# Encoder trunk: low weight parts of the input blocks by ScalarE and an accumulating DMA instead of a VectorE subtraction

## The chip, the cores and the metric

One core of a Trainium2 chip runs the whole program in one launch. The metric is device microseconds of one execution. Before the change it is 1680.81 us, the median of three runs (1680.68 to 1682.55).

## The reference

Two layers of a streaming encoder trunk run over 656 tokens (16 learned and 512 prompt tokens, and 8 running streams of 16). Each layer does

```
h    = rmsnorm(x, g_mix)
proj = h @ w_in                      # 1024 -> 3072: 24 blocks of 128 columns, the heads' inputs
oa   = diff_attention(qa, ka, va)    # 4 heads, two softmaxes each, chunk mask, cached keys
ob   = silu(layernorm(dwconv31(glu)))  # 256 channels, 31 taps
oc   = hgrn2(q, log_f, k, v, S0)     # 4 heads, 64x64 state
x    = x + concat(oa, ob, oc) @ w_out
x    = x + (gelu(dwconv3(gate)) * val) @ w_down   # gate, val = rmsnorm(x, g_ffn) @ w_up
```

All of it is float32. The change touches the weights of `h @ w_in` alone.

## The kernel before

**Split products.** TensorE multiplies in fp32r, which keeps fewer bits than float32. So each operand is split into a high part `hi`, its copy in fp32r, and a low part `lo = x - hi`, and `mm3` (L392) issues three matmuls for each 128x128 weight unit and each half of the tokens (328 columns): `whi` with `hi`, `whi` with `lo`, `wlo` with `hi`. One block of 128 output columns has 8 units and 2 token halves, so 48 matmuls. The first token half (24 matmuls) runs before the second; the low part of unit 4, the first unit of the second weight half, is read by matmul 15 of 48.

**Weights of a block.** `w_load` (L364) loads 128x1024 values (512 KB) into one of 4 `raw` buffers through SP's queue. `w_split` (L373) splits them in two halves of 128x512. For each half ScalarE copies `raw` to `whi` (L384), and VectorE writes `wlo = raw - whi` (L385). There are 4 pairs of `whi` and `wlo` buffers, so two blocks fit: a pair comes free when the block that used it has passed its last matmul on that half, and holds the same half of the block after next in order.

**Heads stage.** In each layer the first three blocks are computed together; then a loop runs over blocks n = 3 to 23 (L1188 on): product of block n (`gemm`, result `d_i` in PSUM), eviction by VectorE with the row factor (`evict_r`, L423), `weights` of block n + 1, and between them a step of each generator that has its inputs: the two HGRN2 pairs, the four attention heads (`front`), and the conv module (`back`). The stage is 42 to 311 us in the first layer and 870 to 1137 us in the second.

**Who fills which engine there.** VectorE has the conv's taps as two instructions each (L715 and L716, 18 of the 31 taps after the first), the evictions, the low parts, the masks and merges of HGRN2 and the softmax sums. ScalarE has the high parts, exponentials, squares and PSUM copies. Twelve conv taps per channel tile are made by ScalarE (`cvt`, L722 and L723) and summed by DMAs with `accum_op` add, issued by GpSimd (L725). GpSimd also scales the softmax rows (L528), builds block operands of the streams (`qx`, L644) and does some sums and clears.

**What sets the order.** No order is written out in this stage. A planner replays the program on a model of the engines' costs and gives each engine, in its free moments, the earliest instruction of the program whose inputs are ready; each engine, and each queue of DMA issues, then runs that list in order. So a changed instruction changes the lists of all engines in the stage. In the feed-forward part VectorE and TensorE follow an order that is written out.

Of the kernel before, what the change touches and what calls it, by code (L numbers as in the profile page):

```python
# [9 lines left out]
F32 = mybir.dt.float32  # L10
# [3 lines left out]
ALU = mybir.AluOpType  # L14
# [145 lines left out]
def trunk_kernel(ctx: ExitStack, tc: tile.TileContext, i: dict, o: dict, depth: int = 2):  # L160
# [12 lines left out]
    V, A, G, PE = nc.vector, nc.scalar, nc.gpsimd, nc.tensor  # L173
# [172 lines left out]
    def seq(ins):  # L346

        if start["on"]:
            tc.keep_in_program_order(ins)
            start[ins.ins.engine] = ins.ins  # L350
# [13 lines left out]
    def w_load(w, k0, kt, parts=None):  # L364
        raw = wraw.tile([128, 8, 128], F32, tag="raw", name="raw")
        for a, b in parts or ((0, kt),):
            nc.sync.dma_start(out=raw[:, a:b], in_=w[:, (k0 + a) * 128:(k0 + b) * 128].rearrange("p (k n) -> p k n", n=128))
        return raw

    def unit_s(name):  # L370
        return S(name, F32R)[:, :512].rearrange("p (k n) -> p k n", n=128)

    def w_split(raw, kt, a=0, own=False):  # L373

        half = 4 if kt in (4, 8) else 3
        units = []
        while a < kt:
            n = min(half, kt - a)
            if own:
                hi, lo = unit_s("ghi"), unit_s("glo")  # L380
            else:
                hi = wsp.tile([128, 4, 128], F32R, tag="whi", name="whi")
                lo = wsp.tile([128, 4, 128], F32R, tag="wlo", name="wlo")
            seq(A.copy(hi[:, :n], raw[:, a:a + n]))  # L384
            seq(V.tensor_tensor(out=lo[:, :n], in0=raw[:, a:a + n], in1=hi[:, :n].bitcast(F32), op=ALU.subtract))  # L385
            units += [(hi, lo, m) for m in range(n)]
            a += n
        return units

    def weights(w, k0, kt, own=False):  # L390
        return w_split(w_load(w, k0, kt), kt, 0, own)

    def mm3(ps, unit, rr, ab, first, last):
        whi, wlo, n = unit
# [11 lines left out]
    def gemm(units, ks, rhs, nm, cc=CA, P=PD):  # L406

        return [gemm1(units, ks, rhs, f"{c}_{nm}", cc[c], P) for c in range(2)]
# [11 lines left out]
    def evict_r(ps, r, nm):  # L420
        t = SE(nm)
        for c, (a, b) in enumerate(CA):
            V.tensor_tensor(out=t[:, a:b], in0=ps[c][:, :b - a], in1=r[:, a:b], op=ALU.mult)  # L423
        return t
# [712 lines left out]
    for l in range(depth):  # L1137
        w = i["w_in"][l]
# [3 lines left out]
        col = [cols[a] // 128 + b for a, b in order]  # L1142
        xsrc = i["x"] if l == 0 else xdr
        got, mix = {}, {}
        if l == 0:
            hs = []
            nc.sync.dma_start(out=xs[0][:, :T], in_=i["x"][0])
            raws = [w_load(w[col[n]], 0, 8, ((0, 4),)) for n in range(3)]
            for m in range(1, 4):
                nc.sync.dma_start(out=xs[m][:, :T], in_=i["x"][m])  # L1150
            for n in range(3):
                nc.sync.dma_start(out=raws[n][:, 4:], in_=w[col[n], :, 512:].rearrange("p (k n) -> p k n", n=128))
            for m in range(4, 8):
                nc.sync.dma_start(out=xs[m][:, :T], in_=i["x"][m])
            w3 = []
            start["on"] = True
            for m in range(8):
                hs.append(split(xs[m], par("g_mix", m), f"h{l}{m}"))
                if m == 0:
                    w3 = [w_split(raws[n], 4) for n in range(3)]  # L1160
                if m == 3:
                    w3 = [w3[n] + w_split(raws[n], 8, 4, True) for n in range(3)]
            for m in range(8):
                sq_add(m, E=V)
            start["on"] = False
        r = norm_r(onesd[:, 0], [sq_acc["t"]], f"h{l}")
        ps3 = gemm_group(w3, ks8, hs, f"i{l}")
        with ExitStack() as behind:
            if l == 0:
                for e in (mybir.EngineType.DVE, mybir.EngineType.Activation):  # L1170
                    behind.enter_context(tc.issue_after(start[e]))
            nxt = weights(w[col[3]], 0, 8)
            if l == 0:
                setup()
# [6 lines left out]
        def advance(gens):  # L1181
            for g in list(gens):
                try:
                    next(g)
                except StopIteration:
                    gens.remove(g)

        gpast = None  # L1188
        for n in range(3, 24):
            advance(front)  # L1190
            ps = gemm(nxt, ks8, hs, f"i{l}{n}")
            got[order[n]] = evict_r(ps, r, f"e{l}{n}")
            if n < 23:
                nxt = weights(w[col[n + 1]], 0, 8)
            advance(back)
            if n >= FR:
                advance(front)
            if n >= BK:
                advance(back)
# [5 lines left out]
        while any(k not in mix for k in ka):  # L1205
            advance(front)
            advance(back)
        nxt = weights(wo[0], 0, 6)
        for k in ka:
            mix[k] = split(*mix[k], f"mx{l}{k}")  # L1210
        for m in range(8):
# [4 lines left out]
            nxt = weights(wo[m + 1], 0, 6) if m < 7 else weights(wo[0], 6, 2)  # L1216
# [9 lines left out]
        for m in range(8):  # L1226
# [5 lines left out]
            if m < 7:  # L1232
                nxt = weights(wo[m + 1], 6, 2)
# [20 lines left out]
        for ft in range(2):  # L1254
            ps = ps3[2] if ft == 0 else gemm(weights(wu[NFF + 1], 0, 8), ks8, hs, f"v{l}1", cx, PB)
            a, av = gates.pop(ft)
# [95 lines left out]
        for p in range(1, NFF // 2):  # L1352
            for up in (up_gate, up_val)[1 if p == 1 else 0:]:
                for st in up(p):
# [3 lines left out]
                    while due and due[0][0] <= nprod:  # L1358
                        _, n, j = due.pop(0)
# [66 lines left out]
    with tc.manual_schedule(engines={mybir.EngineType.DVE, mybir.EngineType.PE}):  # L1426

        wl.append(weights(wd[3], f0, nf, True))
        a, b = CF[0]
# [8 lines left out]
        for c, (a, b) in enumerate(CF):  # L1438
            w = b - a
# [50 lines left out]
```

## Time and profile before

| | us |
|---|---|
| median of 3 runs | 1680.81 |
| the profiled execution | 1678.91 |
| its span, first to last instruction | 1677.1 |
| TensorE busy | 1618.5 (97%) |
| VectorE busy | 1245.9 (74%) |
| ScalarE busy | 879.1 (52%) |
| GpSimd busy | 566.8 (34%) |

Busy time is the union of an engine's instructions; matmuls are pipelined, so one of 328 columns shows 0.31 us though the next starts 0.15 us later. In the rows PE is TensorE, PEld its weight loads, DVE VectorE, ACT ScalarE, POOL GpSimd, SP SyncE. L385 is line 385 of the kernel. A name such as wlo<-raw,whi gives what is written and read.

### The profile page before, as it was taken

The page shows a single profiled execution, that of the slowest core. Times are in us where ns is not written, and L with a number is a line of the kernel's source. Part 1 is how long each engine was busy: PE and PEld are TensorE (multiplying, and loading weights), DVE is VectorE, ACT ScalarE, POOL GpSimd, SP SyncE. Part 2 cuts the span into 40 slices and gives each one's busy share as a digit, 9 for nine tenths or more (in the row PEclk, how much of TensorE's full clock was granted, in tenths as well). Part 3 has the DMA queues.
Part 4 walks back from the last instruction along what each step waited for, and adds up shares of the span by engine and source line. Part 5 has one row for each costly group of instructions (what it writes and reads, how often), then busy time and mean ns, then how long its engine had stood idle before and what let it go on. Part 6 is the DMA issues. An engine that isn't in the chain of part 4 may idle for free.

```text
span 1677.1 us, 28733 instructions
## 1 busy us (share of the span) xinstructions
PE 1618.5 (97%) x10774; PEld 1527.1 (91%) x10774; DVE 1245.9 (74%) x2391; ACT 879.1 (52%) x1744; POOL 566.8 (34%) x652
## 2 busy tenths in 40 slices
PE   7999999999899999999999999999999999999997
PEld 7898888898899999999998988888988899999997
DVE  6579985769987767666647898856899777777556
ACT  6656576543554444444437556566545444444444
POOL 0102220007556555554001032100276545554420
PEclk9999999999999999999999999999999999999999
DMA  6236441342144444444532364313511344444453
GB/s 226 74 95 160 111 105 36 113 136 99 45 119 102 102 106 106 105 106 112 190 103 81 95 149 98 99 56 130 179 39 51 98 105 102 102 106 99 108 136 122
DMA packets 75003, 180.56 MB, mean 108 GB/s; under 512 B 12752, under 2 KB 18384, under 8 KB 74864
## 3 DMA queue, kind: packets, MB, share of 16 engines
q1 hardware_dynamic: 62192, 149.36, 27.6%
q0 software_dynamic: 12672, 29.37, 11.2%
q8 instruction: 84, 1.38, 0.3%
q14 instruction: 55, 0.45, 0.1%
HBM read 129.80 MB, written 35.46 MB: 99 GB/s over the span
## 4 chain that ended last, share of the span: by engine, by line
PE 78%; DVE 11%; issue 4%; POOL 3%; ACT 2%; DMA 1%; SPq 0%; POOLq 0%; DVEq 0%; ACTq 0%
PE d_dn L398 16%; PE d_i L398 16%; PE d_v L398 12%; PE d_g L398 12%; PE d_oa L398 5%; PE sc L515 2%; PE e_i L398 1%; PE hl L809 1%; PE po L551 1%; DVE fh L1090 1%; DVE wlo L385 1%; PE d_fin L398 1%; PE e_u L398 1%; DVE wlo L992 1%; POOL gv L1299 1%
## 5 line engine op out<-in xcount | busy, mean ns | idle before, releaser
L398 PE MATMUL d_v<-fh,whi 128*128 128x328 f32 (+1 forms) x1120 | 251.8, 312 | 1.6 <-ACT whi L991 1.6
L384 ACT CAST whi<-raw 128x384 fp32r<-128x384 f32 (+2 forms) x243 | 132.6, 548 | 208.8 <-PE d_i L398 76.5
L398 PE MATMUL d_g<-fh,whi 128*128 128x328 f32 (+1 forms) x1008 | 226.5, 312 | 0.3 <-ACT whi L991 0.3
L398 PE MATMUL d_i<-hi_h,whi 128*128 128x328 f32 x672 | 219.3, 326 | 0.0
L398 PE MATMUL d_i<-lo_h,whi 128*128 128x328 f32 x672 | 213.9, 318 | 0.0
L398 PE MATMUL d_i<-hi_h,wlo 128*128 128x328 f32 x672 | 212.9, 317 | 0.0
L398 PE MATMUL d_dn<-hi_g,wlo 128*128 128x328 f32 (+1 forms) x640 | 199.8, 312 | 2.8 <-DVE wlo L385 2.8
L398 PE MATMUL d_dn<-hi_g,whi 128*128 128x328 f32 (+1 forms) x640 | 200.2, 313 | 1.9 <-ACT hi_g L356 1.7
L398 PE MATMUL d_dn<-lo_g,whi 128*128 128x328 f32 (+1 forms) x640 | 200.1, 313 | 1.8 <-DVE lo_g L357 1.8
L385 DVE TENSOR_TENSOR wlo<-raw,whi 128x384 fp32r<-128x384 f32 (+2 forms) x243 | 170.9, 717 | 30.5 <-ACT whi L384 22.7
L398 PEld LDWEIGHTS d_v<-fh,whi 128*128 128x128 f32 x1120 | 189.3, 189 | 2.2 <-ACT whi L991 2.2
L992 DVE TENSOR_TENSOR wlo<-wcb,whi 128x512 fp32r<-128x512 f32 x152 | 131.9, 868 | 74.9 <-ACT whi L991 72.3
L398 PE MATMUL d_v<-fh,wlo 128*128 128x328 f32 (+1 forms) x560 | 175.5, 313 | 3.3 <-DVE wlo L992 3.3
L398 PEld LDWEIGHTS d_g<-fh,whi 128*128 128x128 f32 x1008 | 170.4, 189 | 0.5 <-ACT whi L991 0.5
L398 PE MATMUL d_g<-fh,wlo 128*128 128x328 f32 (+1 forms) x504 | 157.8, 313 | 2.3 <-DVE wlo L992 2.3
L985 POOL TENSOR_TENSOR wcb<-raw 128x512 f32<-128x512 f32 x76 | 109.6, 1442 | 127.8 <-DMA raw<-in_w_up 80.2
L992 DVE TENSOR_TENSOR wlo<-raw,whi 128x512 fp32r<-128x512 f32 x114 | 114.8, 1008 | 50.7 <-ACT whi L991 50.5
L991 ACT CAST whi<-wcb 128x512 fp32r<-128x512 f32 x152 | 93.7, 620 | 110.6 <-PE d_g L398 33.3
L398 PEld LDWEIGHTS d_i<-hi_h,whi 128*128 128x128 f32 x672 | 127.5, 190 | 10.1 <-issue 5.6
L398 PEld LDWEIGHTS d_i<-lo_h,whi 128*128 128x128 f32 x672 | 127.6, 190 | 3.8 <-issue 1.3
L398 PEld LDWEIGHTS d_i<-hi_h,wlo 128*128 128x128 f32 x672 | 127.2, 189 | 3.0 <-issue 1.3
L398 PEld LDWEIGHTS d_dn<-hi_g,wlo 128*128 128x128 f32 x640 | 121.1, 189 | 3.5 <-DVE wlo L385 3.5
(394 smaller groups left out, 4026.9 us busy)
## 6 DMA issues: line engine op xcount, KB each, us to landing
raw<-in_w_up SPq DMA_DIRECT2D x88, 512.0 KB, 3.7
raw<-in_w_in SPq DMA_DIRECT2D x45, 512.0 KB, 3.7
raw<-in_w_down SPq DMA_DIRECT2D x48, 384.0 KB, 3.8
x_scr<-x SPq DMA_DIRECT2D x24, 328.0 KB, 3.2
x_scr<-dd POOLq DMA_DIRECT2D x24, 328.0 KB, 4.5
x<-x_scr SPq DMA_DIRECT2D x24, 328.0 KB, 4.4
x_scr<-dd POOLq DMA_DIRECT2D x24, 320.0 KB, 4.6
cvb<-cvt POOLq DMA_DIRECT2D x20, 328.0 KB, 5.0
```

The lines of the kernel that those rows point to most:

```text
L384: seq(A.copy(hi[:, :n], raw[:, a:a + n]))
L385: seq(V.tensor_tensor(out=lo[:, :n], in0=raw[:, a:a + n], in1=hi[:, :n].bitcast(F32), op=ALU.subtract))
L398: PE.matmul(ps[:, :b - a], lhsT=ww[:, n], rhs=r[:, a:b], start=first and j == 0, stop=last and j == 2)
L515: PE.matmul(ps[:, o0:o0 + w], lhsT=q[64 * c:64 * c + 64, q0:q0 + 128], rhs=k[64 * c:64 * c + 64, n * w:(n + 1) * w], start=True, stop=True)
L551: PE.matmul(po[:, :128], lhsT=vt[:, j * 128:(j + 1) * 128], rhs=aT[:, j * 128:(j + 1) * 128], start=j == 0, stop=False)
L809: PE.matmul(ps[:, c * 128:(c + 1) * 128], lhsT=kk[:, 16 + 128 * c:144 + 128 * c], rhs=both(m0 + 64 * c, 64), start=True, stop=True)
L985: G.tensor_tensor(out=t, in0=x, in1=y, op=op)
L991: A.copy(hi, x)
L992: V.tensor_tensor(out=lo, in0=x, in1=hi.bitcast(F32), op=ALU.subtract)
L1090: V.tensor_tensor(out=lo, in0=x, in1=hi.bitcast(F32), op=ALU.subtract)
L1299: G.tensor_tensor(out=v[:, a0:TP], in0=v[:, a0:TP], in1=a[:, a0:TP], op=ALU.mult)
```

## The change

For blocks 4 to 22 of each layer the low part of the second weight half is no longer subtracted by VectorE. ScalarE writes `wlo = -1 * whi`, and GpSimd issues a DMA that adds `raw` to `wlo` in place. The first half, blocks 3 and 23, the first three blocks and all other weights stay as they are.

```diff
-    def w_split(raw, kt, a=0, own=False):
+    def w_split(raw, kt, a=0, own=False, far=False):
...
             seq(A.copy(hi[:, :n], raw[:, a:a + n]))
-            seq(V.tensor_tensor(out=lo[:, :n], in0=raw[:, a:a + n], in1=hi[:, :n].bitcast(F32), op=ALU.subtract))
+            if far and a > 0:
+
+                A.mul(lo[:, :n], hi[:, :n].bitcast(F32), -1.0)
+                G.dma_start(out=lo[:, :n].bitcast(F32), in_=raw[:, a:a + n], accum_op=ALU.add)
+            else:
+                seq(V.tensor_tensor(out=lo[:, :n], in0=raw[:, a:a + n], in1=hi[:, :n].bitcast(F32), op=ALU.subtract))
...
-    def weights(w, k0, kt, own=False):
-        return w_split(w_load(w, k0, kt), kt, 0, own)
+    def weights(w, k0, kt, own=False, far=False):
+        return w_split(w_load(w, k0, kt), kt, 0, own, far)
...
             if n < 23:
-                nxt = weights(w[col[n + 1]], 0, 8)
+                nxt = weights(w[col[n + 1]], 0, 8, False, n < 22)
```

## Rows read from the trace of the kernel before

**Rows 1.** The page, busy time, share of the span and instructions of each engine.

```profile
PE 1618.5 (97%) x10774; PEld 1527.1 (91%) x10774; DVE 1245.9 (74%) x2391; ACT 879.1 (52%) x1744; POOL 566.8 (34%) x652
```

**Rows 2.** Busy time by stretch: heads stage of both layers (columns in the first line).

```profile
core 0: us, PE busy (x) PEld busy (x) DVE busy (x) ACT busy (x) POOL busy (x), PEclk, DMA share, GB/s
...
42.00:311.00 269.00, 264.13 (x1776) 230.44 (x1775) 210.82 (x532) 166.47 (x364) 43.46 (x75) 0.98 0.37 98
...
870.00:1137.00 267.00, 261.18 (x1777) 227.74 (x1775) 213.60 (x538) 165.01 (x362) 42.79 (x71) 1.00 0.37 97
```

**Rows 3.** TensorE's waits in 870 to 1137: us in total, times, longest.

```profile
PE hvp L774 <- DVE e L423: 2.3, 1, 2.3
PE tm_v L454 <- DVE hsall L922: 1.0, 1, 1.0
...
PE aTq L541 <- ACT hkt L886: 0.6, 1, 0.6
```

**Rows 4.** Timeline of TensorE: start, duration, instruction, idle time before and its releaser.

```profile
168.80 0.44 PE L774 MATMUL hvp<-cst,e 128*128 128x128 f32 x2 [2.31 <-DVE e L423]
...
169.29 2.08 PE L314 MATMUL np_qn<-qsq,cst 128*128 128x328 f32 x4
171.68 1.12 PE L454 MATMUL tm_v<-cst,e 128*128 128x128 f32 x4 [0.30 <-DVE hsall L922]
```

**Rows 5.** Busy time by stretch around the two stalls, with the granted clock.

```profile
169.80:173.20 3.40, 3.10 (x10) 1.95 (x10) 3.21 (x9) 2.27 (x7) 0.00 (x0) 0.50 0.03 5
...
990.00:1003.00 13.00, 9.48 (x57) 7.03 (x58) 12.68 (x31) 5.38 (x14) 0.45 (x3) 1.00 0.24 71
```

**Rows 6.** Timeline of VectorE ahead of the first stall.

```profile
122.66 0.50 DVE L423 TENSOR_TENSOR e<-d_i,r_h 128x328 f32<-128x328 f32 x1 [0.92 <-PE d_i L398]
...
158.74 0.67 DVE L385 TENSOR_TENSOR wlo<-raw,whi 128x512 fp32r<-128x512 f32 x1
...
168.26 0.49 DVE L423 TENSOR_TENSOR e<-d_i,r_h 128x328 f32<-128x328 f32 x1
```

**Rows 7.** Timelines of VectorE and GpSimd at 152 us.

```profile
152.58 2.29 DVE L716 SCALAR_TENSOR_TENSOR cva<-us,cst,cva 128x128 f32<-128x128 f32 x1
...
152.34 2.38 POOL L903 TENSOR_TENSOR hvx<-hvt,cst 128x512 f32<-128x512 f32 x2
```

**Rows 8.** Groups by line, 42 to 311: busy us, mean ns of one, idle before.

```profile
L385 DVE TENSOR_TENSOR wlo<-raw,whi 128x512 fp32r<-128x512 f32 x38 | 27.2, 716 | 3.5 <-ACT whi L384 3.2
L384 ACT CAST whi<-raw 128x512 fp32r<-128x512 f32 x38 | 23.3, 618 | 40.3 <-PE d_i L398 36.2 <-issue 3.5 <-ACT qo L800 0.5
...
L722 ACT ACTIVATE cvt<-u,cst 128x528 f32<-128x528 f32 x20 | 14.5, 726 | 0.0
L716 DVE SCALAR_TENSOR_TENSOR cva<-us,cst,cva 128x128 f32<-128x128 f32 x36 | 14.4, 400 | 0.0
...
L725 POOL DMA_DIRECT2D cvb<-cvt x10 | 9.7, 1069 | 15.2 <-ACT cvt L723 14.9
```

**Rows 9.** The conv's accumulating DMAs of 328 KB in 42 to 311, issue to landing.

```profile
DMA to landing us min/median/max: 3.7/5.0/7.3
```

**Rows 10.** Timelines of ScalarE, TensorE and GpSimd around blocks 6 and 14.

```profile
64.68 1.14 ACT L384 CAST whi<-raw 128x512 fp32r<-128x512 f32 x2
...
74.42 0.32 PE L398 MATMUL d_i<-hi_h,wlo 128*128 128x328 f32 x1
...
145.16 0.62 ACT L384 CAST whi<-raw 128x512 fp32r<-128x512 f32 x1 [1.18 <-PE d_i L398]
...
158.32 0.31 PE L398 MATMUL d_i<-hi_h,wlo 128*128 128x328 f32 x1
...
67.24 0.28 POOL L644 COPY qx<-e 64x128 f32<-64x128 f32 x1 [22.86 <-DVE e L469]
...
149.87 1.87 POOL L725 DMA_DIRECT2D cvb<-cvt  x2 [5.61 <-ACT cvt L723]
```

## The prediction, made before the change was run

> **What bounds the kernel now.** The page's busy times come first: TensorE is busy for 1618.5 of 1677.1 us, VectorE for 1245.9 [rows 1]. That leaves TensorE 58.6 us of idle time in the whole program, and the question is how much of it lies where the change acts. Busy time by stretch answers it: in the first layer's heads stage TensorE is busy for 264.13 of 269.00 us, in the second layer's for 261.18 of 267.00 [rows 2]. Only 4.87 + 5.82 = 10.7 us stand open there. So the stage is bound by TensorE, and whatever VectorE is spared, no more than 10.7 us can come back, plus what a lowered clock costs. VectorE is the second limit: 210.82 and 213.60 us busy, a mean of 79%; ScalarE has 62%, GpSimd 16% [rows 2].
>
> The waits say who is late when TensorE does stop. In the second layer the largest is a transpose of HGRN2's values that waits 2.3 us for an eviction by VectorE, then 1.0 us at the transposes of an attention head, also behind VectorE [rows 3]. The first layer's timeline has the same pair, 2.31 and 0.30 us [rows 4]. Behind the first pair the granted clock stands at 0.50, that is 1.2 instead of 2.4 GHz, for 3.4 us; in the second layer, after the same wait, it stays at 1.00 [rows 5]. The four norm matmuls in the slow stretch take 2.08 us [rows 4]. Half of 3.4 us, 1.7 us, is what the first layer's dip costs at most, were TensorE at work throughout.
>
> Why VectorE is late is in its own timeline. From the eviction at 122.66 us on it has hardly an idle moment, and the eviction for which TensorE waits starts at 168.26 us, behind conv taps and low parts [rows 6]. In that stretch one tap instruction takes 2.29 us where the mean of its group is 0.40; it starts 0.24 us after GpSimd begins two sums that last 2.38 us [rows 7, 8]. So part of VectorE's lateness, about 1.9 us at this instruction, comes from sharing something with GpSimd's arithmetic, and the change leaves those sums where they are.
>
> **What is removed.** 19 subtractions per layer (blocks 4 to 22), 38 in all, each 0.716 us in the mean [rows 8]: 19 x 0.716 = 13.6 us of VectorE per layer. Nearly all of it lies beside TensorE's work and is worth nothing. It counts where VectorE runs without a break ahead of a late result: between 122.66 and 168.26 us four second halves stand in its list, those of blocks 12 to 15, the last at 158.74 us [rows 6]. Taken at 0.67 us each they are 2.7 us. The last one surely lies in the way, which gives 0.7 us as the lower end. The earlier three count as far as the planner doesn't put other work in their place; it will put conv taps there, but the taps are a fixed number, so those moved ahead are missing later. I take three of the four, 2.0 us. The stall of the first layer falls from 2.31 + 0.30 to 0.6, that of the second from 2.3 + 1.0 to 1.3. The clock dip followed one of two equal stalls, so I count half of its 1.7 us, 0.85. Gain: 2.0 + 0.85 + 2.0 = 4.9 us. Its bounds are 0.7 + 0.7 = 1.4 us, and 2.6 + 1.7 + 3.3 = 7.6 us when both pairs and the dip go.
>
> **What ScalarE gets.** 19 multiplications of 128x512 per layer. The trace has no such instruction; below it stands the copy of that shape, 0.618 us, above it the scaled copy of 528 columns, 0.726 us [rows 8]. The operation is the latter's kind, so I take 0.71: 13.5 us per layer, and ScalarE's share goes from 62% to 67%. It runs right behind a copy that ScalarE had to wait for TensorE to start (36.2 of 40.3 us of idle time ahead of those copies [rows 8]), and what it pushes back by 0.7 us is the next thing in ScalarE's list. TensorE waits for ScalarE in one named place per layer, 0.6 us [rows 3]. So the cost lies between nothing and one push in front of such a place in each layer, 1.4 us; a gain is excluded, since ScalarE loses nothing. I take 0.7 us for both layers.
>
> **What GpSimd gets.** 19 DMA issues per layer at 1.07 us, the mean of the conv's [rows 8]: 20 us on an engine with 43.46 of 269 us busy [rows 2]. Each issue waits for its multiplication, and behind it in GpSimd's list stand the conv's accumulating issues, the softmax scaling and the `qx` copies; the issue is placed by the planner when its input is ready, so that those behind lose about 1.1 us each. TensorE doesn't wait on any of them in the rows of waits, so I put this at nothing; without that cover it would be 1.1 us for each one that TensorE meets.
>
> **The new path of the low part.** The multiplication is done 0.7 us after the high part, and the transfer lands 3.7 to 7.3 us after its issue begins, median 5.0, for 328 KB [rows 9]; 256 KB should not be slower, so I use these as they stand. From the end of the high part to the landing that is 4.4 to 8.0 us. What is there is read from two kinds of block. The tightest is block 6: its two high parts end at 64.68 + 1.14 = 65.82 us and TensorE reads the low part at 74.42, 8.6 us later. In the fast rhythm, block 14: the high part ends at 145.78, the read is at 158.32, 12.5 us later [rows 10]. The other 17 blocks, read the same way, leave 12.1 us or more. So every landing is in time if GpSimd is free to issue, and the step costs nothing. Its cover is 8.6 - 8.0 = 0.6 us in the worst case of block 6, and about 4 us elsewhere.
>
> The raw buffer is held until the transfer has read it, some 4 us longer. Its next load is for the block four later; with blocks at 9 us and a load of under 5 us this is covered, and SP's list behind it has only loads of caches and stores. Nothing is counted.
>
> Sum: 4.9 - 0.7 = 4.2 us faster. The profiled execution took 1678.91 us, so 1674.7 us on its scale; the median of the runs is 1.9 us above it, and the forecast on that scale is 1676.6 us.
>
> **Rivals.** *The gaps come back elsewhere.* TensorE is 98% busy in both stages, and the planner orders all engines anew; the idle 10.7 us have ten causes or so, and a new order makes new ones. For it speaks that VectorE's list was late by GpSimd's sums, which remain; against it, that VectorE has 13.6 us less in each layer. Time: 1680.8, within 2 us.
>
> *Late low parts, the slower side.* One mechanism: GpSimd's list is in order, and the issue stands behind an instruction that waits for VectorE. At block 6 GpSimd sits 22.86 us in front of a `qx` copy that starts at 67.24; an issue placed behind the four copies (0.28 us each) begins at 68.4, lands at 72.1 to 75.7, and TensorE wants it at 74.42 [rows 9, 10]: up to 1.3 us late. At block 14 an issue behind the conv's two that begin at 149.87 [rows 10] starts at 151.7 and lands at 155.4 to 159.0, against 158.32: up to 0.7 us late. Each such stall may bring the clock dip of 1.7 us as well. With one to three blocks per layer that is 2 x (1 to 3) x (0.7 to 3.0), 1.4 to 18 us; I price it at 6 us net of the gain, 1686.8. It decides once the path from high part to landing exceeds 8.6 us at block 6 or 12 us at the others. For it: VectorE, for which GpSimd waits, is the engine that runs late here. Against it: the multiplications are ready some time ahead of those waits' ends, and the planner lists by readiness.
>
> The Trainium skill has a rule that speaks for this rival: by "SBUF — State Buffer" (section "SBUF: two separate sides") GpSimd cannot write the descriptors of a DMA that it issues while VectorE holds the port pair they share in a two-port mode. By that rule issues among VectorE's dense work would be stretched and land late. The trace doesn't bear it out: the conv's issues stand among VectorE's dense work and land after 3.7 to 7.3 us [rows 9], which is in time.
>
> *ScalarE in the way.* If the multiplications push more than one gating copy per layer, at 0.7 us each and five per layer, 7 us are lost and 2 us gained: 1685.8.
>
> *A better packing.* If the lighter VectorE lets nearly all of the open 10.7 us go, about 9 us: 1671.8.
>
> **How the numbers follow.** Forecast 50%, gaps elsewhere 20%, late low parts 15%, ScalarE in the way 7%, better packing 8%. 0.2% is 3.4 us, about what a measurement of this kernel tells from no change. The forecast's own range, 1.4 to 7.6 us less the cost, is 1673 to 1680; some three fifths of it, 31%, lie beyond 3.4 us. Faster: 31 + 8 = 39%, rounded to 40. Slower: 15 + 7, and 1 from the second case, 23%. Same: 37%. The range takes in most of the better packing and the cheaper part of the two slower cases: 1671 to 1686.
>
> **What would show it.** Right: VectorE's group of 128x512 low parts falls from 38 to 19 in each stage's rows; ScalarE shows 19 scaled copies of 0.65 to 0.75 us; GpSimd 39 issues instead of 20, about 1 us each; issue to landing 3.5 to 7 us; TensorE's busy share of both stages rises, the 2.3 us wait before the transposes shrinks. Wrong: waits of `d_i` on a landing among TensorE's waits (late low parts); waits of `d_i` or small matmuls on ScalarE (ScalarE in the way); the same idle total with other names (gaps elsewhere). If TensorE's busy time itself changes by more than 2 us with the clock at 1.00, something is at work that these rows don't show.

## The result, and the profile after

The changed kernel takes 1673.17 us, median of five runs (1671.20 to 1675.67); the kernel before, timed beside it, 1682.18 us (five runs). The ratio is 0.995 with a 95% interval of 0.9936 to 0.9964: 6 to 11 us faster. The forecast was 4.2 us faster.

The profiled execution took 1674.07 us, its span is 1672.1 us; the page's line of busy times, to be read against [rows 1]:

```profile
PE 1615.0 (97%) x10774; PEld 1525.0 (91%) x10774; DVE 1210.2 (72%) x2353; ACT 901.3 (54%) x1782; POOL 601.3 (36%) x690
```

VectorE has 38 instructions and 35.7 us less, ScalarE 38 more and 22.2 us more, GpSimd 38 more and 34.5 us more. The groups of the first layer's heads stage, as in [rows 8], and behind them the landing of the new transfers, as in [rows 9]:

```profile
L390 DVE TENSOR_TENSOR wlo<-raw,whi 128x512 fp32r<-128x512 f32 x20 | 13.8, 688 | 3.9 <-ACT whi L384 3.9
L721 DVE SCALAR_TENSOR_TENSOR cva<-us,cst,cva 128x128 f32<-128x128 f32 x36 | 13.2, 369 | 0.0
L387 ACT ACTIVATE wlo<-whi 128x512 fp32r<-128x512 f32 x18 | 11.4, 631 | 0.5
L388 POOL DMA_DIRECT2D wlo<-raw x18 | 15.8, 876 | 75.6 <-ACT wlo L387 61.8 <-ACT qo L805 5.9 <-PE np_qn L314 4.5
...
DMA to landing us min/median/max: 3.3/3.3/6.2
```

(The rows show 18 of the 19; that of block 4 is issued at 35.90 us, ahead of the stretch.) The multiplication takes 0.63 us, the issue 0.88 us, the landing 3.3 to 6.2 us. The heads stages by stretch, from the first product behind the three joint blocks to the first of the output product, in the kernel before and then in the changed one:

```profile
42.40:309.90 267.50, 263.34 (x1776) 230.28 (x1775) 209.72 (x528) 165.37 (x363) 43.46 (x75) 0.99 0.37 97
870.00:1135.80 265.80, 260.72 (x1775) 227.53 (x1773) 212.40 (x534) 163.81 (x361) 42.79 (x71) 1.00 0.36 95
```

```profile
44.80:307.70 262.90, 260.27 (x1775) 228.25 (x1774) 195.82 (x510) 175.92 (x381) 58.92 (x93) 0.99 0.49 118
868.00:1130.50 262.50, 259.31 (x1776) 227.02 (x1775) 197.84 (x516) 174.66 (x379) 58.49 (x89) 1.00 0.47 115
```

So the profiled gain is here: 4.6 and 3.3 us, 7.9 in sum. The spans differ by 5.0 us only, mainly because the part ahead of the first stage took 44.8 instead of 42.4 us; over all the kernels profiled here it takes 42.4 to 44.8 us, whether they have the change or not. Of the 7.9 us 3.4 are idle time of TensorE and 4.5 its busy time. Of TensorE's waits in the second layer (us in total, times, longest) the first of [rows 3] is down to 0.15 us, too short for these rows, and the second is halved:

```profile
PE tm_v L459 <- DVE e L428: 0.8, 2, 0.4
PE aTq L546 <- ACT hkt L891: 0.5, 1, 0.5
PE tm_v L461 <- DVE hsall L927: 0.5, 1, 0.5
```

In the first layer 0.14 of the 2.31 us are left, and the clock stays up behind them: the stretch that answers to [rows 5] shows 1.00 where 0.50 stood, and the four norm matmuls take 1.44 instead of 2.08 us [rows 4].

```profile
167.60:171.00 3.40, 2.77 (x15) 1.85 (x16) 3.08 (x12) 2.78 (x8) 0.00 (x0) 1.00 0.65 148
```

Why the eviction is in time is in the timelines of GpSimd and VectorE (start, duration, instruction, idle time before), which answer to [rows 6, 7]:

```profile
157.13 0.86 POOL L388 DMA_DIRECT2D wlo<-raw  x1 [2.02 <-ACT wlo L387]
157.69 2.37 POOL L908 TENSOR_TENSOR hvx<-hvt,cst 128x512 f32<-128x512 f32 x2
159.69 0.95 POOL L912 MEMSET hsall<- 128x640 f32 x1
160.28 1.36 POOL L938 TENSOR_TENSOR s<-s,tot 128x512 f32<-128x512 f32 x1
```

```profile
157.31 1.29 DVE L903 TENSOR_TENSOR hst<-hsi,cst 128x512 f32<-128x512 f32 x2
158.51 2.10 DVE L905 TENSOR_REDUCE otok<-hst 128x64 f32<-128x512 f32 x2
160.54 1.25 DVE L721 SCALAR_TENSOR_TENSOR cva<-us,cst,cva 128x128 f32<-128x128 f32 x1
...
167.17 0.49 DVE L428 TENSOR_TENSOR e<-d_i,r_h 128x328 f32<-128x328 f32 x1
```

The two `hvx` sums run at 157.69, not at 152.34 [rows 7]. Part of that is the later start of the stage: counted from its first product (42.41 us before, 44.80 after) they begin at 112.9 instead of 109.9 us, 3.0 us later, and in the second layer 3.7 us later. (These sums, as the prediction calls them, are elementwise products; the name is kept here.) They stand in GpSimd's list behind the issue for block 15's low part, which waited 2.02 us for its multiplication. Beside them VectorE now has `hst`, whose input lies in PSUM, and a reduction. Both keep their length (two in 1.29 and in 2.10 us; before, one took 0.68 and 1.08 us, alone). Only one tap instruction is stretched, by 0.91 us over the usual 0.34; before, two were, by 1.95 (the one in [rows 7]) and by 1.30 over 0.76, this one beside the `s` sum:

```profile
154.80 2.06 DVE L715 SCALAR_TENSOR_TENSOR cva<-u,cst,cva 128x528 f32<-128x528 f32 x1
```

```profile
154.92 1.37 POOL L933 TENSOR_TENSOR s<-s,tot 128x512 f32<-128x512 f32 x1
```

Counted from the stage's first product, the eviction that `hvp` waits for begins 3.5 us earlier than before.

### The profile page after: what moved, and what is told of

The parts are those of the page before. It is cut to its first block, busy times and chain, and to the rows that moved or that the text cites. A ratio compares the mean times of both kernels' runs of the same rounds, so it can differ in the third digit from the quotient of the medians.

```text
span 1672.1 us, 28858 instructions
## 1 busy us (share of the span) xinstructions
PE 1615.0 (97%) x10774; PEld 1525.0 (91%) x10774; DVE 1210.2 (72%) x2353; ACT 901.3 (54%) x1782; POOL 601.3 (36%) x690
## 4 chain that ended last, share of the span: by engine, by line
PE 76%; DVE 11%; POOL 4%; issue 4%; ACT 3%; DMA 3%; SPq 0%; POOLq 0%; DVEq 0%; ACTq 0%
PE d_i L403 16%; PE d_dn L403 16%; PE d_v L403 12%; PE d_g L403 12%; PE d_oa L403 5%; PE sc L520 2%; PE e_i L403 1%; DMA x<-x_scr 1%; PE po L556 1%; DVE fh L1095 1%; PE hl L814 1%; PE d_fin L403 1%; DMA cvb<-cvt 1%; POOL gv L1304 1%; DVE wlo L997 1%
## 5 line engine op out<-in xcount | busy, mean ns | idle before, releaser
L390 DVE TENSOR_TENSOR wlo<-raw,whi 128x384 fp32r<-128x384 f32 (+2 forms) x205 | 142.2, 711 | 28.9 <-ACT whi L384 21.6
```

## The experiments

Each ratio is against the kernel before, timed on the same chip in the same set. Two theories were set against each other. **Load:** what counts is VectorE's free time, 13.6 us more per layer. **Collision:** what counts is which VectorE instructions run beside the `hvx` and `s` sums on GpSimd; the change moved the sums by putting an issue that waits ahead of them. The expectations name the theories as they stood before each run.

**One part of the blocks.** Five blocks (12 to 16), whose low parts stand ahead of the late eviction, and then the others:

```diff
-                nxt = weights(w[col[n + 1]], 0, 8, False, n < 22)
+                nxt = weights(w[col[n + 1]], 0, 8, False, 11 <= n < 16)
```

> The new low part is used for blocks 12 to 16 alone (5 of 19 per layer), those whose subtractions stood in VectorE's unbroken list ahead of the late eviction. The whole change gave 9 us. Theory S (only the subtractions ahead of the late results count): most of it is here, 5 to 8 us faster, and the 2.3 us waits of the transposes are under 1 us. Theory E (every subtraction taken from VectorE is worth about the same): 5/19 of 9, 2.4 us. Theory O (the planner's new order did it, not the load): any amount, with no relation to which blocks.

Measured: 0.9985 [0.9973, 0.9996].

```diff
+                nxt = weights(w[col[n + 1]], 0, 8, False, n < 11 or 16 <= n < 22)
```

> The complement: blocks 4 to 11 and 17 to 22 (14 of 19 per layer) take the new low part, blocks 12 to 16 are subtracted on VectorE. Theory S: 0 to 3 us faster than before, and the 2.3 us waits stand. Theory E: 14/19 of 9, 6.6 us faster. Theory O: no relation.

Measured: 1.0014 [1.0005, 1.0023]. TensorE's waits in the first layer, of these five blocks and then of the others:

```profile
PE sc L520 <- DVE att L821: 1.2, 1, 1.2
PE tm_v L461 <- DVE hsall L927: 1.0, 1, 1.0
PE tm_v L459 <- DVE e L428: 0.8, 1, 0.8
```

```profile
PE hvp L779 <- DVE e L428: 2.3, 1, 2.3
PE sc L520 <- DVE att L821: 0.9, 1, 0.9
```

With the five, the wait of `hvp` is gone, but a third of the gain is all that comes: the waits for `att` and `hsall` are now near 1 us (0.3 us for `hsall` before, and `att` not among its waits). With the other 14 blocks the wait stays and the kernel is a little slower, though VectorE is spared 10 us per layer: those 10 us buy nothing.

**Relief without the new path.** The second halves' low parts are left out: `wlo` is a cleared tile, so there is no subtraction, multiplication or transfer.

```diff
+    zlo = const.tile([128, 4, 128], F32R, name="zlo")
...
-                lo = wsp.tile([128, 4, 128], F32R, tag="wlo", name="wlo")
+                lo = zlo if far and a > 0 else wsp.tile([128, 4, 128], F32R, tag="wlo", name="wlo")
...
-            if far and a > 0:
...
-            else:
+            if not (far and a > 0):
```

> Leaves out the low parts of the second halves of blocks 4 to 22: neither subtraction nor multiplication nor DMA; TensorE multiplies with a cleared tile in their place, so its work is the same. This is the relief of VectorE without what ScalarE, GpSimd and the DMAs pay for it. If the new path costs nothing (the prediction's step), 8 to 10 us faster than before, as the change itself; if it costs the 0.7 to 1.4 us that the prediction gave ScalarE, 10 to 11 us. If the change's gain came from the low part being ready earlier by its new way, this would not differ either, but the first-half waits would move; if from the order alone, any amount.

Measured: 0.9981 [0.9972, 0.9991]. It has all of the relief and none of the cost, and yet gains only a third of what the change does. Its timelines of VectorE and GpSimd, and its waits:

```profile
152.41 2.56 DVE L720 SCALAR_TENSOR_TENSOR cva<-us,cst,cva 128x128 f32<-128x128 f32 x1
...
168.69 0.48 DVE L427 TENSOR_TENSOR e<-d_i,r_h 128x328 f32<-128x328 f32 x1
```

```profile
152.44 2.38 POOL L907 TENSOR_TENSOR hvx<-hvt,cst 128x512 f32<-128x512 f32 x2
```

```profile
PE hvp L778 <- DVE e L427: 2.6, 1, 2.6
```

The sums stay at 152 us, a tap beside them takes 2.56 us, and the wait is 2.6 us. Without the subtractions the late eviction is hardly earlier, 0.5 us counted from the stage's first product: the planner fills their place with taps.

**The new path without the relief.** The subtractions stay; the multiplication and the transfer go to a tile that nobody reads.

```diff
+                d = wsp.tile([128, 4, 128], F32, tag="dum", name="dum", bufs=1)
+                A.mul(d[:, :n], hi[:, :n].bitcast(F32), -1.0)
+                G.dma_start(out=d[:, :n], in_=raw[:, a:a + n], accum_op=ALU.add)
+            seq(V.tensor_tensor(out=lo[:, :n], in0=raw[:, a:a + n], in1=hi[:, :n].bitcast(F32), op=ALU.subtract))
```

> All subtractions stay on VectorE; besides, ScalarE's multiplication and the accumulating DMA are done for blocks 4 to 22 into a tile that nobody reads. This is the new path's cost without the relief. Theory S with a free path: within 1.5 us of before. If ScalarE's 12 us per layer or the DMAs are in the way: 2 to 7 us slower. Theory O (a new order gives the gain without any relief): faster by several us.

Measured: 1.0042 [1.0029, 1.0054], 7 us slower. The second layer's stage alone is 8.2 us longer, and what stands out in it is the second layer's other pair of sums, at 1075 us:

```profile
1074.86 2.35 POOL L907 TENSOR_TENSOR hvx<-hvt,cst 128x512 f32<-128x512 f32 x2
```

```profile
1075.07 4.28 DVE L389 TENSOR_TENSOR wlo<-raw,whi 128x512 fp32r<-128x512 f32 x1
```

```profile
1076.00:1090.00 14.00, 10.29 (x40) 6.11 (x37) 11.70 (x25) 5.26 (x13) 3.28 (x5) 0.63 0.32 81
```

A subtraction of 0.68 us takes 4.28 us beside the sums, TensorE stops for 3.6 us at 1076.6 and then runs at a mean of 0.63 of its clock. So this kernel doesn't measure the path's price, as it was meant to; it shows the same collision in another place.

**One block against all others.** The change a second time, then for block 15 alone, and for all but block 15:

> The changed kernel once more, beside the runs of before on this chip, as the measure for the others: 6 to 9 us faster; mean granted clock of its runs 0.992 to 0.994 against 0.990 of before.

Measured: 0.9943 [0.9931, 0.9956], like the first time (0.995); the mean granted clock is 0.9932.

```diff
+                nxt = weights(w[col[n + 1]], 0, 8, False, n == 14)
```

> Only block 15 of each layer takes the new low part: one subtraction per layer less. Theory C (the gain comes from GpSimd's list: the DMA issue of block 15 stands ahead of GpSimd's two hvx sums and makes them wait some 5 us, so that they no longer run beside VectorE's conv taps and stretch them by 3 us, and the late eviction, the 2.3 us stall and the clock dip behind it go): 2 to 5 us faster, and the taps' stretch falls from 3.3 us to under 1 us. Theory S or E (VectorE's load): 1/19 of the relief, under 1 us.

Measured: 0.997 [0.9959, 0.9981], 5 us for one block of the 19. GpSimd's list, and the tap beside it:

```profile
157.71 0.86 POOL L388 DMA_DIRECT2D wlo<-raw  x1 [3.40 <-ACT wlo L387]
158.27 2.37 POOL L908 TENSOR_TENSOR hvx<-hvt,cst 128x512 f32<-128x512 f32 x2
```

```profile
158.07 1.29 DVE L903 TENSOR_TENSOR hst<-hsi,cst 128x512 f32<-128x512 f32 x2
159.27 2.11 DVE L905 TENSOR_REDUCE otok<-hst 128x64 f32<-128x512 f32 x2
161.28 1.08 DVE L721 SCALAR_TENSOR_TENSOR cva<-us,cst,cva 128x128 f32<-128x128 f32 x1
```

```diff
+                nxt = weights(w[col[n + 1]], 0, 8, False, n < 22 and n != 14)
```

> All but block 15 take the new low part (18 of 19 subtractions per layer less), so no issue stands ahead of the hvx sums. Theory C: the 2.3 us stalls and the 3.3 us stretch of the taps are back, and at most 3 us are gained. Theory E: 18/19 of the gain, 6 to 8 us. Theory S (the four subtractions ahead of the stall): three of four gone, 4 to 7 us.

Measured: 0.998 [0.9969, 0.999], the gain of relief alone (0.9981). No issue stands between the conv's and the sums now, these begin at 153.94 us, a subtraction beside them is stretched, and TensorE waits:

```profile
153.94 2.38 POOL L908 TENSOR_TENSOR hvx<-hvt,cst 128x512 f32<-128x512 f32 x2
```

```profile
154.08 2.79 DVE L390 TENSOR_TENSOR wlo<-raw,whi 128x512 fp32r<-128x512 f32 x1
```

```profile
169.11 0.44 PE L779 MATMUL hvp<-cst,e 128*128 128x128 f32 x2 [1.79 <-DVE e L428]
```

That this gain equals that of the low parts left out also says something of the new path's price: with the sums in such a place in both, 18 multiplications and transfers per layer are no slower than none, to within some 2 us, the half-width of either interval. It is no proof that the path is free: the waits of `hvp` are 2.2 us shorter in sum here, which could hide a price of that size.

**The sums taken away.** The kernel before, all subtractions in place, with only the `hvx` and `s` sums given to VectorE:

```diff
-            G.tensor_tensor(out=vx[:, :512].rearrange("p (s v) -> p s v", s=8),
+            V.tensor_tensor(out=vx[:, :512].rearrange("p (s v) -> p s v", s=8),
...
-        G.tensor_tensor(out=s1[:, :512].rearrange("p (s v) -> p s v", s=8),
+        V.tensor_tensor(out=s1[:, :512].rearrange("p (s v) -> p s v", s=8),
```

> The kernel before, with nothing of the change: only GpSimd's sums of HGRN2 (two hvx and one s per pair) are done by VectorE instead. VectorE gets 3 x 0.7 us more per pair, and no sum of GpSimd runs beside its taps there. Theory C: the stretch of 3.3 us is gone, the 2.3 us stalls shrink under 1 us, 2 to 5 us faster. Theory S and E: VectorE has more to do, so the same or up to 3 us slower.

Measured: 0.9951 [0.9939, 0.9964]: 8 us, nearly the whole gain, and nothing of the change. VectorE has 12 instructions more, of 0.68 us each; it is busy for 1241.7 us against 1245.9 all the same, since the stretches go. Load would have made it slower. VectorE's own `hvx`, and the tap behind it at its usual length:

```profile
158.51 0.68 DVE L903 TENSOR_TENSOR hvx<-hvt,cst 128x512 f32<-128x512 f32 x1
...
162.30 0.35 DVE L716 SCALAR_TENSOR_TENSOR cva<-us,cst,cva 128x128 f32<-128x128 f32 x1
```

As the planner orders all engines anew, and the sums of the other pair are moved too, this isn't the collision at 152 us alone.

**Both together, and both halves.** The change with the sums on VectorE; then the change for both weight halves (`if far:` in place of `if far and a > 0:`); then both halves with the sums on VectorE.

> The change, and beside it the sums of HGRN2 (hvx and s) on VectorE instead of GpSimd. Theory of the collision: with the sums gone from GpSimd no tap can be stretched by them, whatever the new issues do to GpSimd's list; the change then adds only the relief of VectorE, which was 3 us with the low parts left out. So it should come to between the change alone and 3 us below it, 1669 to 1673 (ratio 0.992 to 0.995 against before), with no stretched tap above 0.3 us in the stages and no wait of hvp above 1 us. Theory of the load (what counts is VectorE's free time, 13.6 us more per layer): the sums put work back on VectorE, so it is 1 to 3 us slower than the change alone. If the two gains were of two kinds and independent, 8 + 9 us would add to 1664.

Measured: 0.9974 [0.9964, 0.9984]. A miss: no instruction ahead of `hvp` is stretched and `hvp` doesn't wait, but it gains less than either edit alone. The planner puts a low part at 230.42 us ahead of the mask for which the scores wait, and the same in the second layer, where the clock falls behind it:

```profile
230.42 0.78 DVE L390 TENSOR_TENSOR wlo<-raw,whi 128x512 fp32r<-128x512 f32 x1
231.12 0.76 DVE L821 COPY_PREDICATED att<-cst,hl 128x256 f32<-128x256 int32 x2
```

```profile
PE sc L520 <- DVE att L821: 1.2, 1, 1.2
```

```profile
1050.00:1063.00 13.00, 11.45 (x47) 8.04 (x47) 10.23 (x31) 6.85 (x16) 2.20 (x5) 0.74 0.56 142
```

> Both halves of blocks 4 to 22 by ScalarE and the accumulating DMA: 38 subtractions per layer off VectorE instead of 19, 27 us instead of 13.6. Theory of the collision: the second 13.6 us buy at most the idle time that is left, 6 us in each stage, and GpSimd's list gets 38 waits, so that the place of the hvx sums is again by chance: 1668 to 1678. Theory of the load: twice the relief, another 5 to 9 us below the change, 1664 to 1668. Theory of late low parts: the first half is read by the second matmul that uses it, 3 us sooner than the second half, so block 6 (3 to 4 us of slack for the second half) would stall for up to 1 us in each layer, to be seen as a wait of d_i on a landing.

Measured: 0.9995 [0.9984, 1.0006]. VectorE is spared twice as much, and the gain is gone:

```profile
158.99 0.86 POOL L388 DMA_DIRECT2D wlo<-raw  x1 [2.49 <-ACT cvt L728]
159.56 2.37 POOL L908 TENSOR_TENSOR hvx<-hvt,cst 128x512 f32<-128x512 f32 x2
```

```profile
159.62 4.03 DVE L721 SCALAR_TENSOR_TENSOR cva<-us,cst,cva 128x128 f32<-128x128 f32 x1
...
168.43 0.48 DVE L428 TENSOR_TENSOR e<-d_i,r_h 128x328 f32<-128x328 f32 x1
```

```profile
168.97 0.44 PE L779 MATMUL hvp<-cst,e 128*128 128x128 f32 x2 [3.22 <-DVE e L428]
```

With more issues in GpSimd's list the sums begin 4.3 us later than in the changed kernel, counted from the stage's first product (117.2 against 112.9 us), when VectorE is done with `hst` and its reductions; they meet a tap, it takes 4.03 us, and TensorE waits 3.22 us. No first half landed late.

> Both halves as above and the sums on VectorE. Theory of the collision: no stretched tap, so it should not be slower than both halves alone, and 1666 to 1672. Theory of the load: the sums are 5 us of VectorE per layer against 13.6 us spared, so about 2 us slower than both halves alone.

Measured: 0.9946 [0.9933, 0.9958], 1671.40 us. The only edit against the kernel above is who does the sums, and it is worth 8 us. It is level with the change itself (0.9943 and 0.995), and no version tried here beat that.

**GpSimd subtracts.** The same relief, but by a GpSimd subtraction in place of multiplication and transfer:

```diff
+            if far and a > 0:
+                G.tensor_tensor(out=lo[:, :n], in0=raw[:, a:a + n], in1=hi[:, :n].bitcast(F32), op=ALU.subtract)
```

> The second half's low part of blocks 4 to 22 is subtracted by GpSimd itself, instead of ScalarE and a DMA: VectorE is spared the same 13.6 us per layer, but GpSimd now has 19 more sums of 128x512 with both inputs in SBUF. Theory of the collision: each lasts 1 to 1.5 us and stretches the tap beside it by about its own length, so VectorE loses as much as it is spared; stretched taps of 10 to 25 us per layer in sum, and a time of 1681 to 1692. Theory of the load: as the change, 1671 to 1675.

Measured: 1.0042 [1.0029, 1.0056], 7 us slower, as the collision had it.

```profile
L386 POOL TENSOR_TENSOR wlo<-raw,whi 128x512 fp32r<-128x512 f32 x18 | 24.8, 1378 | 68.9 <-ACT whi L384 62.4 <-PE np_kn L314 6.3
```

```profile
166.55 1.36 DVE L719 SCALAR_TENSOR_TENSOR cva<-us,cst,cva 128x128 f32<-128x128 f32 x1
```

A GpSimd subtraction at 166.47 us stretches the tap at 166.55 from 0.34 to 1.36 us. Stretches of over 0.3 us, against the median of the same line and shape, add up to 10.7 and 9.5 us in the two stages, against 6.0 and 5.2 before. VectorE still has 15.6 us less in all than before (1230.3 against 1245.9), so that it lost less than it was spared, against the expectation, and yet TensorE's idle time in the two stages is 5.7 us more: where the stretches fall counts. GpSimd doesn't come off free here: one of its subtractions takes 1.27 to 1.80 us.

All kernels in one table: the stretch (us over the usual length, summed over VectorE's instructions stretched by over 0.3 us in the 25 us ahead of `hvp`) and the wait of `hvp`, for layer 1 and layer 2, and the length of both heads stages together, of the profiled executions:

| kernel | ratio | stretch, us | wait of `hvp`, us | both stages, us |
|---|---|---|---|---|
| before | 1 | 3.25, 3.26 | 2.31, 2.34 | 533.3 |
| the change (twice) | 0.995, 0.9943 | 0.91, 0.78 | 0.14, 0.15 | 525.3, 524.8 |
| blocks 12 to 16 | 0.9985 | 0.59, 0.60 | none | 531.4 |
| the other 14 | 1.0014 | 3.53, 3.05 | 2.28, 1.81 | 534.4 |
| low parts left out | 0.9981 | 3.52, 3.53 | 2.60, 2.60 | 531.4 |
| subtraction and path | 1.0042 | 3.53, 3.46 | 2.69, 2.71 | 540.7 |
| block 15 alone | 0.997 | 0.74, 0.61 | 0.14, none | 528.2 |
| all but block 15 | 0.998 | 3.00, 2.11 | 1.79, 1.23 | 531.9 |
| before, sums moved | 0.9951 | 0, 0 | none | 525.5 |
| change, sums moved | 0.9974 | 0, 0 | none | 528.5 |
| both halves | 0.9995 | 3.69, 2.49 | 3.22, 2.04 | 531.9 |
| both halves, sums moved | 0.9946 | 0, 0 | none | 524.0 |
| GpSimd subtracts | 1.0042 | 3.02, 2.95 | 1.90, 1.88 | 540.5 |

The wait is 1.2 us or more wherever the stretch is above 2 us, and 0.15 us at most wherever it is below 1. The time follows it only in part: the other waits differ too, as in blocks 12 to 16 and in the change with the sums moved. The length of the two stages follows the times to within some 2 us, so the differences arise there. What moves the sums shows too: where they run on GpSimd, counted from the stage's first product, they begin at 108.6 to 109.9 us in the first layer if GpSimd has nothing to do for block 15's low part, and at 112.8 to 117.2 if it has. Whether that helps depends on what VectorE runs at that time. Block 15's issue alone gives about 5 us and the relief alone about 3; no run splits the 9 us of the change further.

## Why the prediction was right or wrong

The direction was right and the time lies in the range; the size of the gain was half of what was measured, and the reason given for its largest term fell.

**The step that failed** is "comes from sharing something with GpSimd's arithmetic, and the change leaves those sums where they are". The sharing was read rightly; the second half is wrong. The prediction counted 19 issues on GpSimd and asked who waits behind them, but looked among TensorE's waits only, and put it "at nothing". Behind the issue for block 15 stand the two sums, and their delay, 3.0 us within the stage, is what takes the stretch off the taps: 3.25 to 0.91 us. That the time still lies in the range owes something to luck: the largest term came near its size for another reason than the one given.

**The stalls.** The term was 2.0 us a layer. Measured, the two waits fall from 2.61 to 0.52 us in the first layer (the one of `hvp` is then 0.14, too short for the rows above) and from 3.3 to 0.5 in the second, 2.1 and 2.8. TensorE's idle time in the stages fell by less, from 4.16 to 2.63 and from 5.08 to 3.19 us, since waits of the scores (`sc`) of about 0.5 us came up. The rest of the 7.9 us is busy time, 3.1 us in the first layer and 1.4 in the second. The prediction allowed for 2 us of it at a clock of 1.00, which the second layer keeps to; in the first the stretches at a granted clock of 0.50 shrink from 7.9 us (42.4 to 46.9 and 169.8 to 173.2) to 3.6 (44.8 to 48.4), worth some 2 us by estimate. What the other 2.4 us of busy time are isn't shown. The size of the term was near, but the cause was not "three of the four" subtractions: with all of them out and the sums in place the wait was 2.60 us. The planner filled the room, as the rival of the gaps said.

**The clock.** Half of one dip, 0.85 us, was too little. The mean granted clock of the timed runs is 0.9902 for the kernel before and 0.9932 for the change, in the set in which the change ran again; were TensorE at work throughout, 0.0030 x 1677 = 5 us of the 9 would be the clock's, an estimate and the most that it can be. The profiled execution of before, which the prediction read, had 0.993, above the mean of its kernel, and that of the change had 0.993 too. That fits with the profiled executions lying 4.8 us apart and the medians 9. How many of the dips follow from the `hvp` waits isn't settled: kernels without that wait have 0.9909 to 0.9932, those with it 0.9872 to 0.9915.

**VectorE, ScalarE, GpSimd.** 13.6 us less per layer on VectorE was right (27.2 to 13.8 us in the group). ScalarE's instruction takes 0.63 us, near the lower bound; the 0.7 us of cost was not seen: TensorE's wait for `hkt` went from 0.6 to 0.5 us, and no other wait for ScalarE came up in the stages, so that *ScalarE in the way* fell too. The issue takes 0.88, not 1.07 us.

**Late low parts**, the slower rival, fell. Landings of 3.3 to 6.5 us were within the bound, and the least time from a landing to its first read is 3.9 us in the first layer and 2.9 in the second, both at block 6. The rule of the Trainium skill that was weighed there ("SBUF — State Buffer", section "SBUF: two separate sides": issues starve beside VectorE's two-port work) stays untested: the 18 issues of a stage take 0.85 to 0.92 us each among VectorE's dense work, but no row shows whether any of that work is in a two-port mode, and the prediction took the rule to hold for all dense work. What the same section of the Trainium skill says of the lock agrees with the trace in which instructions are hit: by it a VectorE instruction with both inputs in SBUF shuts out, or waits for, a GpSimd instruction that reads SBUF, whichever starts first going ahead. Taps and subtractions went from 0.34 to 4.03 and from 0.68 to 4.28 us beside the sums, `hst` with its input in PSUM did not (0.65 us). Who goes ahead the trace doesn't bear out: with the low parts left out the tap began 0.03 us ahead of the sums, as recorded, and it waited all the same. The prediction had the tap of 2.29 us before it and drew no forecast from it.

**Gaps elsewhere** and **a better packing** were both seen: the first in other kernels, both halves (0.9995) and the change with the sums moved, the second in the change itself, whose time is nearer to the 1671.8 us of that rival than to the forecast.

## What to carry to other kernels

When an in-order engine gets a new instruction that waits, follow everything behind it, also what nobody seems to wait for: a delayed sum can stop colliding with another engine, or begin to. Before an edit is credited with the time that it spares, the same time should be spared without its side effects (here: left out altogether, it bought a third) and the side effect be made alone (here: one issue of the 19 brought half of the gain, the sums moved to VectorE most of it). An instruction that takes several times the mean of its group is a place to look at first, and the cure may be to move its neighbour.

## What was not expected of the hardware

A tap instruction of 128x128 took 0.34 us alone and 1.25, 2.29, 2.56 or 4.03 us by how it met GpSimd's sums, and the sums themselves kept 2.37 to 2.38 us for two in all of these: VectorE paid, these sums didn't. In the case of 4.03 us the tap began 0.06 us after the sums and was over at 163.65 us, behind both and the `s` sum that began at 162.14: it was held through all three.
